# A decoder segment on one core: the small part of every fourth weight chunk formed by an accumulating DMA in SBUF

## The chip, the core and the metric

The kernel runs on one core of a Trainium2 chip. The metric is the time of one execution on the device, in microseconds (us), the median of several runs. The engines are named as the profile names them: PE is the matrix engine TensorE and PEld its weight loads, DVE is VectorE, ACT is ScalarE, POOL is GpSimd; SP is SyncE, which here only issues DMAs. SBUF is the on-chip working memory, PSUM the memory into which PE accumulates.

## The reference, cut to what matters

Two layers work on 256 tokens of 2048 features in float32. Layer 0 mixes tokens with a gated linear recurrence (HGRN2), layer 1 with differential attention over keys and values made from layer 0's output; each is followed by an MLP of 8192 hidden features and a gated embedding:

```python
x = x + o.reshape(b, s, A_WIDTH) @ a_w_out[j]                    # o: HGRN2 mixer, or attention with b_w_out
h = rms_norm(x, ln_mlp[i])
x = x + jnp.square(jax.nn.relu(h @ mlp_up[i])) @ mlp_down[i]
gate = jax.nn.sigmoid(rms_norm(x, ln_ple[i]) @ ple_gate[i])
x = x + gate * (p[i] @ ple_proj[i])
```

With few tokens nearly all the work is matrix products with large float32 weights, each of which is read once.

## The kernel before

The products are made in float32r, a shortened float32, and to keep the accuracy each operand is split into a large part and a small one: `hi` is the value rounded to float32r, and `lo` is the value minus `hi`. A product is then the sum of three: hi times hi, lo times hi and hi times lo.

Weights come in **chunks** of 512 KB, 128 partitions by 1024 elements: two blocks of 128 input features by 512 output features. `chunk` (L91 to L98) brings one: SP loads `raw` (L93), ACT rounds it into `hi` (L96), and DVE subtracts into `lo` (L97). There are four buffers for `raw` and three each for `hi` and `lo`, so a chunk can be prepared only when PE has finished the chunk three before it. 872 chunks are brought in one execution.

`group_b` (L119) takes eight chunks for 512 output features, with the weights stationary. Each chunk serves two pairs of feature blocks, eight matmuls a pair in `mm_b` (L108): for each block, `hi` against both parts of the activations side by side (L114, 512 columns), then `lo` against their large part alone (L116, 256 columns). The second pair starts only when two chunks have gone through the first, so PE takes chunk 0 first pair, chunk 1 first pair, chunk 0 second pair, chunk 1 second pair, and from chunk 2 on both pairs of a chunk. `group_a` (L133) does the same with the tokens stationary, twelve matmuls of 512 columns a chunk (L143 to L145), for the values of the two mixers (four groups of `w_in`, four of `w_v`).

At the end of a group its sums are taken from PSUM. In an up projection (`ev_up`, L523) that is a copy on ACT (L235), an addition and a scaled maximum on DVE (L236, L526), a square on ACT (L527) and the split of the result (L102 on ACT, L103 on DVE). In a down projection it is two additions on DVE (L244, L245). Norms, the mixers and the gates go on beside the stream of chunks, a step after each chunk (`pump`).

No order is written out by hand: a scheduler sorts the program's instructions into one queue for each engine by its own estimate of when each can start, and each engine takes its queue in order. PE thus waits at the first instruction whose operand is not there. POOL has almost nothing to do: constants, masks, four memsets of `accd` (L338) and, once, four loads of 512 KB of `x` (L508).

## Time and profile before

| | before |
|---|---|
| median of 2 runs | 2548.05 us (2545.41 to 2550.69) |
| the profiled execution | span 2545.3 us; no other time is given for it |
| granted PE clock, mean | 0.999 |
| DMA, mean | 184 GB/s, 467.24 MB in all |
| chunks | 872 |

The span runs from the first to the last instruction of one execution taken by the profiler. "Busy" counts an engine's instructions, without waits; a busy PE is not PE at its peak. In rows of waits one reads who waited, for whom, how long in total, how often, and the longest. In rows of the timeline one reads the start, the length, the engine, the line, what is written from what, and in brackets how long the engine had been idle and what ended that. "Landing" is the time from a DMA's issue until its data are there. In rows by stretch, each engine has its busy time and its count, then come PE's granted clock, the share of time that the DMA engines were busy, and GB/s.

### The profile page before, as it was taken

The page shows a single profiled execution, that of the slowest core. Times are in us where ns is not written, and L with a number is a line of the kernel's source. Part 1 is how long each engine was busy: PE and PEld are TensorE (multiplying, and loading weights), DVE is VectorE, ACT ScalarE, POOL GpSimd, SP SyncE. Part 2 cuts the span into 40 slices and gives each one's busy share as a digit, 9 for nine tenths or more (in the row PEclk, how much of TensorE's full clock was granted, in tenths as well). Part 3 has the DMA queues.
Part 4 walks back from the last instruction along what each step waited for, and adds up shares of the span by engine and source line. Part 5 has one row for each costly group of instructions (what it writes and reads, how often), then busy time and mean ns, then how long its engine had stood idle before and what let it go on. Part 6 is the DMA issues. An engine that isn't in the chain of part 4 may idle for free.

```text
span 2545.3 us, 36254 instructions
## 1 busy us (share of the span) xinstructions
PE 2529.0 (99%) x14350; PEld 2199.1 (86%) x14350; DVE 1686.0 (66%) x2064; ACT 1360.0 (53%) x1703; POOL 9.7 (0%) x19
## 2 busy tenths in 40 slices
PE   8999999999999999999999999999999999999998
PEld 7888888888888888888888888888888888888887
DVE  7898887665555555556687686566555555556666
ACT  7666666444344354455576566555435445435555
POOL 0000000000000000000000000000000000000000
PEclk9999999999999999999999999999999999999999
DMA  7555554666666666666656555566666656666665
GB/s 234 173 158 166 165 174 151 214 191 189 190 189 189 187 189 190 191 189 191 183 184 186 179 154 159 169 190 185 187 183 195 185 184 197 187 188 190 190 188 159
DMA packets 128570, 467.24 MB, mean 184 GB/s; under 512 B 14288, under 2 KB 14928, under 8 KB 128400
## 3 DMA queue, kind: packets, MB, share of 16 engines
q1 hardware_dynamic: 127440, 461.95, 59.2%
q0 software_dynamic: 816, 2.89, 0.4%
q8 instruction: 112, 1.84, 0.3%
q14 instruction: 58, 0.48, 0.1%
q10 hardware_dynamic: 144, 0.09, 0.0%
HBM read 462.77 MB, written 2.10 MB: 183 GB/s over the span
## 4 chain that ended last, share of the span: by engine, by line
PE 98%; DVE 1%; DMA 0%; ACT 0%; issue 0%; SPq 0%; ACTq 0%
PE mmps L114 58%; PE mmps L116 29%; PE mmps L145 2%; PE mmps L144 2%; PE mmps L143 2%; PE smps L382 1%; PE mmps L573 1%; PE smps L216 1%; PE mmps L575 0%; DMA xa<-x_t 0%; PE smps L345 0%; PE smps L661 0%; PE smps L689 0%; DVE lo L97 0%; PE smps L413 0%; PE smps L415 0%
## 5 line engine op out<-in xcount | busy, mean ns | idle before, releaser
L114 PE MATMUL mmps<-big,hi 128*128 128x512 f32 x6336 | 2221.7, 395 | 0.1
L116 PE MATMUL mmps<-big,lo 128*128 128x256 f32 x6336 | 1770.1, 279 | 0.4 <-DVE lo L97 0.4
L97 DVE TENSOR_TENSOR lo<-raw,hi 128x1024 fp32r<-128x1024 f32 x872 | 1066.1, 1224 | 796.4 <-ACT hi L96 795.2
L96 ACT CAST hi<-raw 128x1024 fp32r<-128x1024 f32 x872 | 914.1, 1049 | 1005.9 <-PE mmps L114 926.2
L114 PEld LDWEIGHTS mmps<-big,hi 128*128 128x128 f32 x6336 | 1189.4, 188 | 278.8 <-DVE u L236 0.4
L116 PEld LDWEIGHTS mmps<-big,lo 128*128 128x128 f32 x6336 | 1191.1, 188 | 2.5 <-DVE lo L97 0.7
L143 PE MATMUL mmps<-hi,big 128*128 128x512 f32 x256 | 102.3, 399 | 0.0
L144 PE MATMUL mmps<-lo,big 128*128 128x512 f32 x256 | 100.1, 391 | 0.3 <-DVE lo L97 0.3
L145 PE MATMUL mmps<-hi,big 128*128 128x512 f32 x256 | 100.3, 392 | 0.0
L235 ACT COPY t<-mmps 128x512 f32<-128x512 f32 (+1 forms) x114 | 65.1, 572 | 24.0 <-PE mmps L116 22.3
L527 ACT ACTIVATE u<-u 128x512 f32<-128x512 f32 x64 | 40.3, 629 | 48.7 <-DVE u L526 48.7
L145 PEld LDWEIGHTS mmps<-hi,big 128*128 128x128 f32 x256 | 48.1, 188 | 10.3
L144 PEld LDWEIGHTS mmps<-lo,big 128*128 128x128 f32 x256 | 48.2, 188 | 9.7 <-DVE lo L97 0.5
L143 PEld LDWEIGHTS mmps<-hi,big 128*128 128x128 f32 x256 | 48.2, 188 | 9.1
L236 DVE TENSOR_TENSOR u<-mmps,t 128x512 f32<-128x512 f32 x80 | 54.7, 684 | 0.4
L103 DVE TENSOR_TENSOR big<-u,big 128x512 fp32r<-128x512 f32 x80 | 54.7, 683 | 0.2
L244 DVE TENSOR_TENSOR x<-mmps,x 128x512 f32<-128x512 f32 x80 | 54.5, 687 | 0.4
L102 ACT CAST big<-u 128x512 fp32r<-128x512 f32 x80 | 49.4, 618 | 4.8 <-DVE u L423 4.5
L245 DVE TENSOR_TENSOR x<-mmps,x 128x512 f32<-128x512 f32 x80 | 51.2, 680 | 0.0
L526 DVE SCALAR_TENSOR_TENSOR u<-u,rn 128x512 f32<-128x512 f32 x64 | 44.0, 688 | 1.1
L161 ACT ACTIVATE big<-x,sml 128x256 fp32r<-128x256 f32 x96 | 41.0, 498 | 6.4 <-DVE x L245 6.4
L162 DVE SCALAR_TENSOR_TENSOR big<-x,sml,big 128x256 fp32r<-128x256 f32 x96 | 40.2, 481 | 0.0
(157 smaller groups left out, 1067.6 us busy)
## 6 DMA issues: line engine op xcount, KB each, us to landing
raw<-w_up SPq DMA_DIRECT2D x256, 512.0 KB, 4.2
raw<-w_dn SPq DMA_DIRECT2D x256, 512.0 KB, 4.2
raw<-w_in SPq DMA_DIRECT2D x128, 512.0 KB, 3.7
raw<-w_pg SPq DMA_DIRECT2D x56, 512.0 KB, 3.9
raw<-w_ao SPq DMA_DIRECT2D x32, 512.0 KB, 3.8
raw<-w_k SPq DMA_DIRECT2D x32, 512.0 KB, 3.8
raw<-w_q SPq DMA_DIRECT2D x32, 512.0 KB, 3.6
raw<-w_v SPq DMA_DIRECT2D x32, 512.0 KB, 3.6
```

Of the source, the lines that this page charges most:

```text
L96: nc.scalar.copy(hi, raw)
L97: nc.vector.tensor_tensor(lo, raw, hi.bitcast(F32), ALU.subtract)
L103: nc.vector.tensor_tensor(dst[:, k, 1, :], src, dst[:, k, 0, :].bitcast(F32), ALU.subtract)
L114: nc.tensor.matmul(ps[:, ml, :], hi[:, k, m * P:(m + 1) * P], rhs[:, k0 + k].rearrange("p a t -> p (a t)"), start=st, stop=False)
L116: nc.tensor.matmul(ps[:, ml, T:2 * T], lo[:, k, m * P:(m + 1) * P], rhs[:, k0 + k, 0, :], start=False, stop=en)
L143: nc.tensor.matmul(ps[:, tt, :], xs[:, kc, 0, ts], hi[:, k], start=st, stop=False)
L144: nc.tensor.matmul(ps[:, tt, :], xs[:, kc, 0, ts], lo[:, k], start=False, stop=False)
L145: nc.tensor.matmul(ps[:, tt, :], xs[:, kc, 1, ts], hi[:, k], start=False, stop=en)
L235: nc.scalar.copy(t, ps[:, :, T:2 * T])
L236: nc.vector.tensor_tensor(out, ps[:, :, 0:T], t, ALU.add)
L244: nc.vector.tensor_tensor(xm, ps[:, :, 0:T], xm, ALU.add)
L245: nc.vector.tensor_tensor(xm, ps[:, :, T:2 * T], xm, ALU.add)
```

## The change

Three chunks in four stay as they are. For each chunk whose count is a multiple of four, DVE's subtraction is left out. Instead ACT, after rounding `raw` into `hi`, copies `raw` once more with a scale of -1 into `lo`, which leaves minus the rounded value there; then POOL issues a DMA from `raw` to `lo` that adds what it reads to what is there. `lo` ends as `raw` minus `hi`, as before. The DMA reads and writes 128 rows of 4 KB, all within SBUF.

```diff
         lo = wp.tile([P, KCS, CW], F32R, tag="lo", name="lo")
         nc.scalar.copy(hi, raw)
-        nc.vector.tensor_tensor(lo, raw, hi.bitcast(F32), ALU.subtract)
+        turn[0] += 1
+        if turn[0] % 4 == 0:
+            nc.scalar.activation(lo, raw, AF.Copy, scale=-1.0)
+            nc.gpsimd.dma_start(lo.rearrange("p a b -> p (a b)"), raw.rearrange("p a b -> p (a b)"), accum_op=ALU.add)
+        else:
+            nc.vector.tensor_tensor(lo, raw, hi.bitcast(F32), ALU.subtract)
         return hi, lo
 
+    turn = [0]
+
```

The rest of the diff takes comments away. Lines behind the change stand seven further down in the changed kernel: its L102 is the subtraction L97, its L121 and L123 are the matmuls L114 and L116, its L109, L242 and L534 are L102, L235 and L527; L99 is the new copy and L100 the new DMA.

The scheduler makes new queues from this. Three places show what moves. The first is ACT's queue in an up projection, from chunk c=1 of a group to c=4 (each `hi` row is one chunk; the third is c=3). Before:

```order
L96 CAST hi_6758<-raw_6756 128x1024
L235 COPY t_6725<-mmps_6546 128x512
L96 CAST hi_6788<-raw_6786 128x1024
L527 ACTIVATE u_6724<-u_6724 128x512
L235 COPY t_6733<-mmps_6547 128x512
L102 CAST big_6351<-u_6724 128x2x256
L527 ACTIVATE u_6732<-u_6732 128x512
L96 CAST hi_6810<-raw_6808 128x1024
L102 CAST big_6351<-u_6732 128x2x256
L96 CAST hi_6832<-raw_6830 128x1024
```

In the changed kernel, the same chunks:

```order
L96 CAST hi_6819<-raw_6817 128x1024
L242 COPY t_6786<-mmps_6605 128x512
L96 CAST hi_6849<-raw_6847 128x1024
L534 ACTIVATE u_6785<-u_6785 128x512
L242 COPY t_6794<-mmps_6606 128x512
L109 CAST big_6408<-u_6785 128x2x256
L534 ACTIVATE u_6793<-u_6793 128x512
L96 CAST hi_6871<-raw_6869 128x1024
L109 CAST big_6408<-u_6793 128x2x256
L99 ACTIVATE lo_6872<-raw_6869 128x1024
L96 CAST hi_6894<-raw_6892 128x1024
```

The copy into `lo` stands one instruction behind the chunk's `hi`, with the evacuation's last cast between them, and ahead of the next chunk's `hi`.

The second place is PE's queue at the start of the same chunk, c=3 (the numbers of `mmps` are the two pairs of feature blocks). Before:

```order
L114 MATMUL mmps_6740<-big_4048,hi_6810 128x512 [waits Activation_49]
L116 MATMUL mmps_6740<-big_4048,lo_6811 128x256 [waits DVE_49]
L114 MATMUL mmps_6740<-big_4048,hi_6810 128x512
L116 MATMUL mmps_6740<-big_4048,lo_6811 128x256
L114 MATMUL mmps_6740<-big_4048,hi_6810 128x512
```

In the changed kernel:

```order
L121 MATMUL mmps_6801<-big_4081,hi_6871 128x512 [waits Activation_49]
L121 MATMUL mmps_6802<-big_4081,hi_6871 128x512
L123 MATMUL mmps_6801<-big_4081,lo_6872 128x256 [waits DMASW4_49,Activation_49]
L121 MATMUL mmps_6801<-big_4081,hi_6871 128x512
L123 MATMUL mmps_6801<-big_4081,lo_6872 128x256
```

The first use of `lo` now waits for a DMA, and one `hi` matmul of the second pair has been taken ahead of it. At c=7 of a group the order of PE is as before, with one `hi` matmul ahead of the wait.

The third place is SP's queue with the loads of the same stretch (the first row is c=1, the third c=3). Before:

```order
L93 DMA raw_6756<-w_up0 128x1024 [waits DMAHW7_49,DVE_49]
L93 DMA raw_6786<-w_up0 128x1024 [waits DMAHW0_49,DVE_49]
L93 DMA raw_6808<-w_up0 128x1024 [waits DMAHW1_49,DVE_49]
L93 DMA raw_6830<-w_up0 128x1024 [waits DMAHW2_49,DVE_49]
L93 DMA raw_6852<-w_up0 128x1024 [waits DMAHW3_49,DVE_49]
```

In the changed kernel:

```order
L93 DMA raw_6817<-w_up0 128x1024 [waits DMAHW5_49,DMASW2_49]
L93 DMA raw_6847<-w_up0 128x1024 [waits DMAHW0_49,DVE_49]
L93 DMA raw_6869<-w_up0 128x1024 [waits DMAHW2_49,DVE_49]
L93 DMA raw_6892<-w_up0 128x1024 [waits DMAHW1_49,DMASW3_49]
L93 DMA raw_6914<-w_up0 128x1024 [waits DMAHW3_49,DVE_49]
```

The buffer of a chunk whose `lo` is accumulated is given back by the landing of that DMA (DMASW), and the load that takes it is the one five or six chunks later.

## The prediction, made before the result was known

> **What bounds the kernel now.** I read the profile page first: its busy shares, the chain that ended last, and the costliest groups.

> ```profile
> span 2545.3 us, 36254 instructions
> PE 2529.0 (99%) x14350; PEld 2199.1 (86%) x14350; DVE 1686.0 (66%) x2064; ACT 1360.0 (53%) x1703; POOL 9.7 (0%) x19
> ...
> PE 98%; DVE 1%; DMA 0%; ACT 0%; issue 0%; SPq 0%; ACTq 0%
> ...
> L97 DVE TENSOR_TENSOR lo<-raw,hi 128x1024 fp32r<-128x1024 f32 x872 | 1066.1, 1224 | 796.4 <-ACT hi L96 795.2
> L96 ACT CAST hi<-raw 128x1024 fp32r<-128x1024 f32 x872 | 914.1, 1049 | 1005.9 <-PE mmps L114 926.2
> ```

> TensorE (PE) is busy 99% of the span and the chain is PE to 98%. PE is idle for 16 us in all, so no edit that leaves its matmuls alone can win more than 0.6%; VectorE (DVE) and ScalarE (ACT) have room. The waits say who paces whom.

> ```profile
> ACT hi L96 <- PE mmps L114: 926.2, 614, 3.2
> DVE lo L97 <- ACT hi L96: 795.2, 614, 3.6
> ...
> PE mmps L116 <- DVE lo L97: 1.6, 3, 0.9
> ```

> ACT waits for PE 614 times: a chunk's `hi` slot (three of them) must be given back before ACT may round the chunk. DVE waits for ACT. PE itself waits for `lo` 1.6 us in the whole run. So preparation is paced from behind, and what matters is its lead: from the moment a slot comes free to the moment PE needs that chunk's `lo`. The timeline of ACT gives it. First a down projection, where a row of `hi` starts when PE ends the chunk three before:

> ```profile
> 1006.01 1.05 ACT L96 CAST hi<-raw 128x1024 fp32r<-128x1024 f32 x1 [1.72 <-PE mmps L114]
> ...
> 1011.56 1.05 ACT L96 CAST hi<-raw 128x1024 fp32r<-128x1024 f32 x1 [1.72 <-PE mmps L114]
> 1014.33 1.06 ACT L96 CAST hi<-raw 128x1024 fp32r<-128x1024 f32 x1 [1.72 <-PE mmps L114]
> 1018.49 1.05 ACT L96 CAST hi<-raw 128x1024 fp32r<-128x1024 f32 x1 [3.10 <-PE mmps L114]
> 1019.88 1.06 ACT L96 CAST hi<-raw 128x1024 fp32r<-128x1024 f32 x1 [0.33 <-PE mmps L114]
> 1022.65 1.05 ACT L96 CAST hi<-raw 128x1024 fp32r<-128x1024 f32 x1 [1.72 <-PE mmps L114]
> ```

> The one long gap of each group of eight (3.10 us) marks c=3: chunk 0 is given back only after both chunks 0 and 1 went through the first pair of blocks. That tells the rows apart: c=7 starts at 1006.01 and c=3 of the next group at 1018.49. A chunk starts on PE when the chunk before it ends, which is when ACT starts `hi` two chunks later. So c=7 has 1011.56 - 1006.01 = 5.55 us, and c=3 has 1022.65 - 1018.49 = 4.16 us. These two are exactly the chunks whose count is a multiple of four (four chunks of `w_pp` come first, then groups of eight). An up projection has its evacuation on ACT as well:

> ```profile
> 582.72 1.05 ACT L96 CAST hi<-raw 128x1024 fp32r<-128x1024 f32 x1 [1.77 <-PE mmps L114]
> ...
> 588.38 1.05 ACT L96 CAST hi<-raw 128x1024 fp32r<-128x1024 f32 x1 [1.78 <-PE mmps L114]
> ...
> 595.36 0.63 ACT L527 ACTIVATE u<-u 128x512 f32<-128x512 f32 x1 [1.58 <-DVE u L526]
> 595.90 1.04 ACT L96 CAST hi<-raw 128x1024 fp32r<-128x1024 f32 x1
> 596.84 0.61 ACT L102 CAST big<-u 128x512 fp32r<-128x512 f32 x1
> ...
> 599.68 1.05 ACT L96 CAST hi<-raw 128x1024 fp32r<-128x1024 f32 x1 [1.28 <-PE mmps L114]
> ```

> Here c=7 has 588.38 - 582.72 = 5.66 us and c=3 only 599.68 - 595.90 = 3.78 us. PE needs `lo` one `hi` matmul after the chunk's start, and in the changed order two `hi` matmuls after it at c=3; the rows below start 0.23 us apart, so I add 0.23 at c=7 and 0.46 at c=3.

> ```profile
> 1011.48 0.39 PE L114 MATMUL mmps<-big,hi 128*128 128x512 f32 x1
> 1011.71 0.27 PE L116 MATMUL mmps<-big,lo 128*128 128x256 f32 x1
> ```

> **Deadlines** from the start of `hi`: down c=3 4.62, c=7 5.78; up c=3 4.24, c=7 5.89 us.

> **What the change removes.** 218 of the 872 subtractions on DVE, 218 x 1.224 = 267 us of busy time. DVE is not on the path, so this is worth nothing.

> **What it adds on ACT.** 218 copies with scale -1. The nearest row of that shape is the ACTIVATE of 128x1024:

> ```profile
> L225 ACT ACTIVATE pt<-pz x11: 417/1056/1062, 1264.8 to 2539.4; 128x1024 f32<-128x1024 f32 x7, 128x256 f32<-128x256 f32 x4
> ```

> That is 1.06 us, 230 us in all, on an engine that is half idle: no cost by itself. But it stands after `hi` and ahead of the DMA, so it lies on the chunk's path: 1.05 + 1.06 and some 0.03 for handing over, 2.14 us after `hi` starts. In the up projections the changed order has the L102 cast between the two, 0.6 us more at c=3. The next `hi` is pushed back by about 1 us; it has a whole chunk more of lead, and its `lo` on DVE comes 1.2 us behind it, so that delay is hidden.

> **What it adds on POOL and the DMA engines.** 218 accumulating transfers of 512 KB, SBUF to SBUF. No row of this trace shows one; call L the time from its issue on POOL to its landing. The rows around it:

> ```profile
> q1 hardware_dynamic: 127440, 461.95, 59.2%
> ...
> raw<-w_up SPq DMA_DIRECT2D x256, 512.0 KB, 4.2
> raw<-w_v SPq DMA_DIRECT2D x32, 512.0 KB, 3.6
> x<-x_t POOLq DMA_DIRECT2D x4, 512.0 KB, 8.3
> cst<-consts POOLq DMA_DIRECT2D x1, 257.0 KB, 5.2
> ```
> ```profile
> DMA to landing us min/median/max: 3.3/4.0/11.9
> ```
> ```profile
> out<-x SPq DMA_DIRECT2D x1, 512.0 KB, 2.6
> ```
> ```profile
> L508 POOL DMA_DIRECT2D x<-x_t x4: 527/532/536, 445.2 to 446.8; - x4
> ```
> ```profile
> L93 SPq DMA_DIRECT2D raw<-w_up x256: 327/328/328, 508.6 to 2343.3; - x128
> ```

> Lower bound 2.6: a store of 512 KB out of SBUF with nothing beside it. Upper bound 8.3: the loads of `x` from POOL's queue, four at once beside the weights. I take 5.2, built up from the fastest weight load: 3.3 us (the second fence's row is that of all `raw` loads), plus 0.53 - 0.33 = 0.20 for POOL's longer issue, plus one more pass over 512 KB, because an accumulation must also read its destination. The price of a pass: the weight queue's packets took 59.2% of 2545.3 us for 461.95 MB, 3.26 us per MB, 1.71 us for 0.524 MB. The `cst` row, from POOL at half the size, has 5.2 too.

> [...]

> **The lateness.** `lo` is ready 2.14 + L after `hi` starts (2.74 + L for c=3 of an up projection). Less the deadlines: down c=3 L - 2.48, c=7 L - 3.64; up c=3 L - 1.50, c=7 L - 3.75. Nothing behind it on PE can go first, since PE takes its instructions in order, so each is a stall of PE; and the stall also delays the next slot's release, so it is not won back. With L = 5.2: down 2.72 + 1.56 = 4.28 us per group, up 3.70 + 1.45 = 5.15. The token-stationary groups (L143 to L145) take their chunks in plain order:

> ```profile
> 1506.00:1608.00 102.00, 101.93 (x491) 84.25 (x490) 68.03 (x119) 62.32 (x109) 0.00 (x0) 1.00 0.52 161
> ```

> 32 chunks in 102 us, 3.19 each; two chunks and one matmul are 6.61 us of deadline, so L - 4.47 = 0.73, twice a group.

> Groups: the 872 chunks are 107 groups of eight and 16 others. 256 chunks of `w_up` make 32 up groups; 4 groups of `w_in` and 4 of `w_v` are token-stationary; the other 67 I count as down groups. Sum: 67 x 4.28 + 32 x 5.15 + 8 x 1.46 = 286.8 + 164.8 + 11.7 = **463 us**. Against the profiled 2545.3 that is 3008.6; the median of the runs lies 2.7 us above that execution, so **3011 us**.

> **Costed at nothing.** The raw buffer of such a chunk is now freed by the landing, not by DVE. A load five or six chunks later waits for it, and the loads behind it on SP's queue wait too. At the landing PE starts that chunk, so the load has more than three chunks (8.3 us) before its own `hi`, against 4.2 to land; two loads queued behind it are 1.7 us each behind. Were that cover gone, the same stall would pass to `hi`. On POOL the transfers stand behind four memsets of `accd`, which wait for matmuls of heads long since streamed, and behind the four loads of `x`, 2.1 MB at 3.26 us per MB: 7 us once in the run, within the rounding of L.

> **Rivals.** (1) *A copy's price*: the second read overlaps the first and L is 3.3. Then c=7 is in time and c=3 is late by 0.82 and 1.80: 67 x 0.82 + 32 x 1.80 = 113 us, about 2660. For it: the fastest loads; against: both POOL rows. (2) *Not slower*: L at or under 2.68, the point at which 67 x (L - 2.48) + 32 x (L - 1.50) is 51 us, that is 2%. At the bound of 2.6 the sum is 43 us and the time 2591. For it: the lone `out` row; against: SP's issue there is the shorter, it reads once, and DMA engines here are 59% taken. (3) *A slow accumulation*: L = 8.3, lateness down 10.48, up 11.35, token-stationary 7.66 per group: 702 + 363 + 61 = 1127 us, about 3675. For it: the `x` rows; against: those queued four deep. (4) *The clock*: stalls of 3 us and more lower PE's granted clock.

> ```profile
> 2540.00:2545.00 5.00, 0.00 (x0) 0.00 (x0) 1.28 (x3) 1.14 (x3) 0.00 (x0) 0.52 0.07 26
> ```
> ```profile
> 8.57 0.63 PE L114 MATMUL mmps<-pt,hi 128*128 128x512 f32 x1
> 9.00 0.41 PE L116 MATMUL mmps<-pt,lo 128*128 128x256 f32 x1
> 9.21 0.63 PE L114 MATMUL mmps<-pt,hi 128*128 128x512 f32 x1
> ```

> With PE idle at the end, the clock shown is 0.52; after the idle start a pair of matmuls takes 0.64 us instead of 0.35. If c=3 of 99 groups ran slow (2.77 us become 5.07 at worst, but the start was slow for some 3.8 us only, a loss of 1.7): 168 us more, about 3180. Against it: 2.7 to 3.7 us of idleness between long busy stretches. [...]

> **How the numbers follow.** My forecast, L between 4 (2762) and 6.5 (3290), gets 0.55; rival 1, L from 2.7 to 4, 0.17; rival 2, 0.05; rival 3, above 6.5, 0.18; rival 4, 0.05. The range is 2720 (L near 3.8) to 3600 (L near 7.9), which leaves out rival 2, most of rival 1's lower half and the tail of rival 3, some 0.2. About 2% can be told from no change here. Slower by more: everything but rival 2, 0.95; within: 0.04; faster, for which nothing in the profile gives room: 0.01.

> **What would show it.** Right: PE's L116 waits for the DMA of `lo`, two times a group, c=3 about 1.2 us longer than c=7 in down groups and 2.3 in up groups; landing near 5 us; DVE busy near 1420 us, ACT near 1590; clock 1.00. Wrong: no such waits (then L is short), waits on `hi` or on `raw` instead (then the buffers bind), matmuls of 0.63 us in mid-run (the clock), or c=3 and c=7 waits alike.

## The result, and the profile after

| | before | changed |
|---|---|---|
| median of 2 runs | 2548.05 us (2545.41 to 2550.69) | 3125.68 us (3121.60 to 3129.77) |
| ratio, 95% interval | | 1.2273 [1.2219, 1.2328] |
| span of the profiled execution | 2545.3 us | 3119.8 us |
| PE idle (span less busy) | 16.3 us | 419.4 us |
| PE busy | 2529.0 us | 2700.4 us |
| mean granted clock of PE | 1.00 | 0.955 |

The change costs 23%, and the forecast of 3011 us lies 115 us short. The table splits the 574.5 us between the two spans: 403 are PE's idle time and 171 are PE being busy longer with the same 14350 matmuls. The first was forecast, at 463 us; the second was not.

First the page of the changed kernel: busy time of the engines, the two DMA queues (packets, MB, share of 16 engines), the chain that ended last, and the groups that the change touches.

```profile
span 3119.8 us, 37274 instructions
PE 2700.4 (87%) x14350; PEld 2294.5 (74%) x14350; DVE 1448.1 (46%) x1846; ACT 1558.8 (50%) x1921; POOL 197.0 (6%) x237
...
q1 hardware_dynamic: 127440, 461.95, 44.5%
q0 software_dynamic: 32208, 117.19, 20.6%
...
PE 30%; DMA 30%; issue 26%; DVE 7%; ACT 7%; POOLq 0%; ACTq 0%; POOL 0%; SPq 0%; DVEq 0%
...
L121 PE MATMUL mmps<-big,hi 128*128 128x512 f32 x6336 | 2323.1, 409 | 1.6 <-ACT hi L96 1.5
L123 PE MATMUL mmps<-big,lo 128*128 128x256 f32 x6336 | 1832.3, 292 | 389.9 <-DMA lo<-raw 385.9
...
L100 POOL DMA_DIRECT2D lo<-raw x218 | 187.3, 859 | 2882.7 <-ACT lo L99 2590.0
L99 ACT ACTIVATE lo<-raw 128x1024 fp32r<-128x1024 f32 x218 | 229.6, 1053 | 7.9 <-PE mmps L151 7.9
```

The chain that was 98% PE is now 30% DMA. Nearly all idle time of PE (389.9 us) stands before L123, the matmul with `lo`, and its releaser is the new DMA; before L121, the matmul with `hi`, it is 1.6 us. So no `hi` comes late, neither through ACT's longer queue nor through the raw buffers. The queue of the accumulating transfers (with 2.9 MB of others, as before) moves a fifth of the bytes, yet takes 20.6% of the DMA engines against 44.5% for four times as much.

The waits (total, times, longest) and the landing of the new DMA:

```profile
POOL lo L100 <- ACT lo L99: 2590.0, 196, 19.3
...
PE mmps L123 <- DMA lo<-raw: 388.3, 193, 5.1
```
```profile
L100 POOL DMA_DIRECT2D lo<-raw x218: 845/857/901, 20.9 to 3105.1; - x109
...
DMA to landing us min/median/max: 4.5/4.7/6.3
```

193 waits of 2.0 us on average: two for nearly each of the 99 groups with stationary weights. One such chunk, c=3 of a down projection, engine by engine; ACT, POOL, then PE up to the wait of c=7 of the same group.

```profile
1205.05 1.05 ACT L96 CAST hi<-raw 128x1024 fp32r<-128x1024 f32 x1 [3.15 <-PE mmps L121]
1206.01 1.05 ACT L99 ACTIVATE lo<-raw 128x1024 fp32r<-128x1024 f32 x1
```
```profile
1207.35 0.85 POOL L100 DMA_DIRECT2D lo<-raw  x1 [13.12 <-ACT lo L99]
```
```profile
1209.21 0.64 PE L121 MATMUL mmps<-big,hi 128*128 128x512 f32 x2
1212.29 0.35 PE L123 MATMUL mmps<-big,lo 128*128 128x256 f32 x1 [2.44 <-DMA lo<-raw]
1212.48 0.39 PE L121 MATMUL mmps<-big,hi 128*128 128x512 f32 x1
...
1214.23 0.63 PE L121 MATMUL mmps<-big,hi 128*128 128x512 f32 x1
1214.66 0.41 PE L123 MATMUL mmps<-big,lo 128*128 128x256 f32 x1
1214.87 0.63 PE L121 MATMUL mmps<-big,hi 128*128 128x512 f32 x1
...
1226.16 0.36 PE L123 MATMUL mmps<-big,lo 128*128 128x256 f32 x1 [1.20 <-DMA lo<-raw]
1226.36 0.40 PE L121 MATMUL mmps<-big,hi 128*128 128x512 f32 x1
```

Read it as a sum. `hi` starts at 1205.05; POOL begins the DMA 2.30 us later; with the median landing of 4.7 us `lo` is there at about 1212.05; PE goes on at 1212.29, after two `hi` matmuls and a wait of 2.44 us. Then, half a microsecond after the restart, a pair of matmuls takes 0.64 us instead of 0.35, until 1216.3. The windows of the same stretch (us, PE, PEld, DVE, ACT, POOL, then the granted clock) name that: the clock is halved for 3.4 us. After the shorter wait of c=7, 1.20 us, the matmul keeps its 0.40 us.

```profile
1209.20:1212.90 3.70, 1.26 (x8) 0.80 (x7) 1.28 (x2) 1.05 (x1) 0.00 (x0) 1.00 1.01 228
1212.90:1216.30 3.40, 3.40 (x13) 2.91 (x13) 0.00 (x0) 0.08 (x1) 0.00 (x0) 0.50 0.93 292
1216.30:1224.50 8.20, 8.20 (x49) 7.16 (x48) 2.45 (x2) 4.02 (x4) 0.86 (x1) 1.00 0.46 125
```

At c=3 of a group that follows a group of an up projection the wait is longer, since the evacuation of the group before then stands on ACT ahead of the copy. Three waits from the start of the first MLP show it: c=3 of its first group, which follows an output projection and waits like a down group, then c=3 and c=7 of its second group:

```profile
613.73 0.36 PE L123 MATMUL mmps<-big,lo 128*128 128x256 f32 x1 [2.60 <-DMA lo<-raw]
...
641.33 0.36 PE L123 MATMUL mmps<-big,lo 128*128 128x256 f32 x1 [3.48 <-DMA lo<-raw]
653.69 0.36 PE L123 MATMUL mmps<-big,lo 128*128 128x256 f32 x1 [1.06 <-DMA lo<-raw]
```

### The profile page after: what moved, and what is told of

It is laid out like the page before. It is cut to its first block, busy times and chain, and to the rows that moved or that the text cites. A ratio compares the mean times of both kernels' runs of the same rounds, so it can differ in the third digit from the quotient of the medians.

```text
span 3119.8 us, 37274 instructions
## 1 busy us (share of the span) xinstructions
PE 2700.4 (87%) x14350; PEld 2294.5 (74%) x14350; DVE 1448.1 (46%) x1846; ACT 1558.8 (50%) x1921; POOL 197.0 (6%) x237
## 3 DMA queue, kind: packets, MB, share of 16 engines
q1 hardware_dynamic: 127440, 461.95, 44.5%
q0 software_dynamic: 32208, 117.19, 20.6%
## 4 chain that ended last, share of the span: by engine, by line
PE 30%; DMA 30%; issue 26%; DVE 7%; ACT 7%; POOLq 0%; ACTq 0%; POOL 0%; SPq 0%; DVEq 0%
DMA lo<-raw 17%; PE mmps L121 16%; PE mmps L123 9%; DVE lo L102 5%; DMA raw<-w_up 4%; DMA raw<-w_dn 4%; ACT hi L96 4%; ACT lo L99 1%; PE mmps L151 1%; PE mmps L152 1%; DMA raw<-w_in 1%; PE mmps L150 1%; DMA raw<-w_pg 1%; DVE u L533 0%; DVE u L243 0%
## 5 line engine op out<-in xcount | busy, mean ns | idle before, releaser
L121 PE MATMUL mmps<-big,hi 128*128 128x512 f32 x6336 | 2323.1, 409 | 1.6 <-ACT hi L96 1.5
L123 PE MATMUL mmps<-big,lo 128*128 128x256 f32 x6336 | 1832.3, 292 | 389.9 <-DMA lo<-raw 385.9
L123 PEld LDWEIGHTS mmps<-big,lo 128*128 128x128 f32 x6336 | 1256.4, 198 | 465.8 <-issue 287.8
L96 ACT CAST hi<-raw 128x1024 fp32r<-128x1024 f32 x872 | 911.1, 1045 | 1301.6 <-PE mmps L121 1214.4
L121 PEld LDWEIGHTS mmps<-big,hi 128*128 128x128 f32 x6336 | 1236.2, 196 | 279.3 <-ACT hi L96 1.9
L102 DVE TENSOR_TENSOR lo<-raw,hi 128x1024 fp32r<-128x1024 f32 x654 | 799.9, 1224 | 1336.5 <-ACT hi L96 1333.5
L100 POOL DMA_DIRECT2D lo<-raw x218 | 187.3, 859 | 2882.7 <-ACT lo L99 2590.0
L99 ACT ACTIVATE lo<-raw 128x1024 fp32r<-128x1024 f32 x218 | 229.6, 1053 | 7.9 <-PE mmps L151 7.9
L242 ACT COPY t<-mmps 128x512 f32<-128x512 f32 (+1 forms) x114 | 65.1, 572 | 95.7 <-PE mmps L123 92.9
L534 ACT ACTIVATE u<-u 128x512 f32<-128x512 f32 x64 | 40.2, 629 | 48.8 <-DVE u L533 48.8
L109 ACT CAST big<-u 128x512 fp32r<-128x512 f32 x80 | 49.4, 617 | 5.6 <-DVE u L430 5.6
## 6 DMA issues: line engine op xcount, KB each, us to landing
raw<-w_up SPq DMA_DIRECT2D x256, 512.0 KB, 4.5
raw<-w_dn SPq DMA_DIRECT2D x256, 512.0 KB, 4.4
lo<-raw POOLq DMA_DIRECT2D x218, 512.0 KB, 4.7
raw<-w_in SPq DMA_DIRECT2D x128, 512.0 KB, 4.3
raw<-w_pg SPq DMA_DIRECT2D x56, 512.0 KB, 4.3
raw<-w_ao SPq DMA_DIRECT2D x32, 512.0 KB, 4.4
raw<-w_k SPq DMA_DIRECT2D x32, 512.0 KB, 4.4
raw<-w_q SPq DMA_DIRECT2D x32, 512.0 KB, 4.0
```

Source lines behind the costliest of these rows:

```text
L96: nc.scalar.copy(hi, raw)
L99: nc.scalar.activation(lo, raw, AF.Copy, scale=-1.0)
L100: nc.gpsimd.dma_start(lo.rearrange("p a b -> p (a b)"), raw.rearrange("p a b -> p (a b)"), accum_op=ALU.add)
L102: nc.vector.tensor_tensor(lo, raw, hi.bitcast(F32), ALU.subtract)
L121: nc.tensor.matmul(ps[:, ml, :], hi[:, k, m * P:(m + 1) * P], rhs[:, k0 + k].rearrange("p a t -> p (a t)"), start=st, stop=False)
L123: nc.tensor.matmul(ps[:, ml, T:2 * T], lo[:, k, m * P:(m + 1) * P], rhs[:, k0 + k, 0, :], start=False, stop=en)
```

## The experiments

Theory A is the prediction's: a chunk's preparation has a fixed lead, from the release of its slot to PE's first use of `lo`, and the path copy, POOL, DMA is longer than that lead. Rival B: it is the traffic, 114 MB more through the DMA engines beside the weights. Rival C: the copy on ACT and the shifted order of the queues. For the extra busy time: the clock, lowered by the idleness itself, against a cost of the matmuls that has nothing to do with the waits. Each edit is against the changed kernel. Where no interval stands, the time is of one execution; the kernel before had medians of 2545.7 to 2547.1 us beside them.

**e1: DVE adds in the DMA's place.**

```diff
-            nc.gpsimd.dma_start(lo..., raw..., accum_op=ALU.add)
+            nc.vector.tensor_tensor(lo, raw, lo.bitcast(F32), ALU.add)
```

> The copy of minus the large part stays on ACT for every fourth chunk, but DVE adds raw to it instead of the DMA. Theory A (the lead: hi, copy and DMA one after the other take longer than the slots give): copy and addition take 1.05 + 1.23 us behind hi, 3.3 us (3.9 in up projections) against deadlines of 4.2 to 5.9, so no stall: 2545 to 2565 us. Theory B (traffic: 218 more transfers crowd the weight loads): the same. Theory C (the copy on ACT and the changed order of its queue): most of the loss stays, 2900 us or more.

2558.97 us, ratio 1.0048 [1.0032, 1.0065]. The copy is still on ACT (1558.2 us busy) and still ahead of the addition; PE waits for `lo` hardly at all:

```profile
PE 2537.0 (99%) x14350; PEld 2204.6 (86%) x14350; DVE 1686.0 (66%) x2064; ACT 1558.2 (61%) x1921; POOL 9.7 (0%) x19
```
```profile
PE mmps L123 <- DVE lo L100: 1.9, 2, 1.1
```

The copy and its place in ACT's queue cost 0.5%, the DMA the rest. PE's shifted order is not in e1 (two `hi` matmuls in a row stand 6 times in its trace, 112 times in the changed kernel's), but it is in e2b below (112 times), which loses 165 us by all its causes together. So rival C is out as the cause of the loss.

**e2 and e2b: a plain DMA copy.** `accum_op` is removed, so `lo` is `raw` itself and the subtraction is left out for those 218 chunks.

```diff
-            nc.gpsimd.dma_start(lo..., raw..., accum_op=ALU.add)
+            nc.gpsimd.dma_start(lo..., raw...)
```

> The DMA copies raw into lo without adding (lo is then raw, so the small part of every fourth chunk is left out of the computation). Theory A: POOL's issue falls from 0.86 to about 0.53 us and one reading of 512 KB goes (1.3 us), landing about 3.1 us instead of 4.7; stalls at c=3 about 0.9 us in down and 1.9 us in up groups, none at c=7, the clock whole: 2640 to 2700 us. Theory B: the loss shrinks as the DMA engines' time does, by about half, to about 2840 us. If the accumulation itself is not dearer than a copy: 3100 us.

The first time this took 8898.93 us. The matmuls were longer from the first ones on, those before the first changed chunk too, with no wait of PE: the record of a `hi` matmul is 2.8 times as long as in the kernel before (1098 against 395 ns), PE's busy time 3.5 times (8882 against 2529 us).

```profile
L121 PE MATMUL mmps<-big,hi 128*128 128x512 f32 x6336 | 6925.2, 1098 | 0.3 <-ACT hi L96 0.3
```

ACT's rounding and DVE's subtraction kept their 1.05 and 1.22 us, so PE alone was slow. The clock given for this run, 1.00, is no measurement: its trace has no record of the clock, while that of every other run has. A pair of matmuls took 1.26 us (10.71 to 11.97), about twice the 0.64 that it takes at half clock in the changed kernel.

The same program ran again, and beside it one with the same values and no DMA:

> The program of e2 once more (plain copy of raw into lo, the subtraction of every fourth chunk left out). If the 8899 us came from a state of the chip in those two executions: 2640 to 2760 us. If they belong to the program or its values: 8900 us again.

It now took 2711.35 us. The 8899 us belong to those executions and not to the program; what slowed PE there stays open, and nothing is drawn from them. The second run shows what the accumulation itself adds:

```profile
L100 POOL DMA_DIRECT2D lo<-raw x218: 527/527/541, 20.5 to 2696.1; - x109
...
DMA to landing us min/median/max: 2.8/2.9/10.1
```
```profile
PE mmps L123 <- DMA lo<-raw: 106.2, 69, 6.2
```

A plain transfer of the same 512 KB costs POOL 0.53 us instead of 0.86 and lands in 2.9 us instead of 4.7, and the waits fall from 388 to 106 us. By the prediction's formula L = 2.9 gives 67 x 0.42 + 32 x 1.40 = 73 us.

**e10: the same values without a DMA.** `nc.vector.tensor_copy(lo, raw)` in the DMA's place; the subtraction is left out as in e2.

> The same values as in e2 (lo is raw for every fourth chunk, the subtraction left out), but written by DVE: no DMA from POOL. If the slowness of e2 came from the values in the products: 8900 us. If it came from the copying DMA, or from a state of the chip: 2550 to 2570 us, as e1.

2549.77 us. What the values are makes no difference; e2b's 165 us are its transfers.

**e3: the same number of chunks, others of each group** (c=2 and c=6, whose first use is further from the slot's release).

```diff
-        if turn[0] % 4 == 0:
+        if turn[0] % 4 == 3:
```

> The same number of accumulating DMAs, but for the chunks c=2 and c=6 of a group instead of c=3 and c=7. Theory A: both have the long lead (5.55 us), so both stall by about 1.1 us and PE's clock stays at 1.00: 99 groups x 2.1 to 2.2 us, 2755 to 2790 us. Theory B: as many transfers and as many bytes, so as after the change, 3100 us. Theory C: as after the change, 3100 us.

2941.33 us, between what the theories wanted. As many bytes, and 184 us less; the total of the waits for the DMA fell from 388 to 266 us. In the down projections both waits were the 1.0 to 1.2 us that A asks for. In the up projections c=2 still waited 2.3 to 2.7 us, and ACT's timeline shows why:

```profile
607.00 1.05 ACT L96 CAST hi<-raw 128x1024 fp32r<-128x1024 f32 x1 [0.69 <-PE mmps L121]
607.95 0.63 ACT L534 ACTIVATE u<-u 128x512 f32<-128x512 f32 x1
608.48 0.57 ACT L242 COPY t<-mmps 128x512 f32<-128x512 f32 x1
608.95 0.62 ACT L109 CAST big<-u 128x512 fp32r<-128x512 f32 x1
609.47 1.06 ACT L99 ACTIVATE lo<-raw 128x1024 fp32r<-128x1024 f32 x1
```

Three instructions of the evacuation have been put between `hi` and the copy, which starts 2.47 us after `hi` does, where in the changed kernel it is 0.96 in a down group and 1.46 at c=3 behind an up group (633.54 to 635.00). The lead is longer, and so is the path.

**e4: DVE negates** instead of ACT: 0.69 us instead of 1.05, and not behind ACT's evacuation.

```diff
-            nc.scalar.activation(lo, raw, AF.Copy, scale=-1.0)
+            nc.vector.tensor_scalar(lo, raw, -1.0, None, ALU.mult)
```

> DVE instead of ACT writes minus the rounded raw into lo, beside hi and not behind it; the accumulating DMA stays. Theory A: in down groups the DMA is issued 0.8 us earlier, in up groups at c=3 about 1.9 us earlier (no cast and no wait between); the changed order has one hi matmul ahead of lo at c=3 instead of two, 0.23 us back. Waits of PE about 1.9 (down, c=3), 1.8 (up, c=3) and 0.3 us (c=7); 2760 to 2860 us, the spread for how much of the slow clock stays. Theory B: as after the change, 3100 us.

2820.08 us, 306 us less than the changed kernel, as A expected. The DMA is unchanged (landing 4.7), only what stands ahead of it is shorter: c=3 mostly waits 1.4 to 1.6 us in down groups and 1.2 to 1.3 behind up groups (1.9 and 1.8 were expected), and half clock is rarer (21 stretches against 68, a granted clock of 0.984 against 0.955). The output projections and the last three groups of each MLP wait longer, 2.7 to 3.3 us.

```profile
PE mmps L123 <- DMA lo<-raw: 161.7, 123, 5.9
```

**e5: c=7 alone**, every eighth chunk.

```diff
-        if turn[0] % 4 == 0:
+        if turn[0] % 8 == 4:
```

> Accumulating DMAs for c=7 alone, half as many. Theory A: 99 stalls of about 1.06 us, clock 1.00: 2645 to 2670 us. Theory B: half of the loss, about 2835 us. Theory C: half of the loss, about 2835 us.

2769.79 us, 100 us above what was expected. The edit does not choose c=7 all through: four single chunks of the gated embedding come between groups of the second MLP and shift the count, and behind them the chosen chunk is c=3. The first MLP, where it is c=7, lost 47 us over 32 groups, waits of 1.0 to 1.2 us each; the second, with c=7 in its first twelve groups and c=3 in its last seventeen, lost 102. Half the transfers thus cost 223 us of 574, and where in the group they fall sets the price.

**e6: PE kept busy while it waits.** Eight matmuls with a zero operand, which add nothing, after the first `hi` matmul of c=3, in 96 groups: 768 x 0.23 = 177 us of busy time put into the stall (`zero` is a strip of zeros, `warm` is 8 there and 0 elsewhere).

```diff
+                if ml == 0 and k == 0:
+                    for _ in range(warm):
+                        nc.tensor.matmul(ps[:, ml, :], hi[...], zero[...], start=False, stop=False)
```

> As the change, but at c=3 PE multiplies by zeros eight times (8 x 0.23 us, results unchanged) after the hi matmul that stands ahead of the wait for lo. If idleness of PE at c=3 is what lowers its clock, the waits get shorter by these 1.8 us, the matmuls run at full speed, and the time falls by most of the 171 us that the matmuls took longer: 2960 to 3010 us. If the slow clock has another cause (the transfers, the number of stalls at all), or the slow matmuls were only a sign and cost nothing: 3120 us or more.

3053.09 us: 73 us faster with 768 matmuls more, though 43 us above the expected band. The page's busy times, then PE at the end of a stall (in this kernel's numbering L123 takes `hi` and L129 `lo`):

```profile
PE 2772.4 (91%) x15118; PEld 2361.3 (77%) x15118; DVE 1449.2 (47%) x1847; ACT 1558.1 (51%) x1921; POOL 196.8 (6%) x237
```
```profile
752.71 0.36 PE L129 MATMUL mmps<-big,lo 128*128 128x256 f32 x1 [1.09 <-DMA lo<-raw]
752.90 0.39 PE L123 MATMUL mmps<-big,hi 128*128 128x512 f32 x1
```

Without the zeros PE is busy 2772 - 177 = 2595 us, 105 less than in the changed kernel. What is left of the wait is 1.09 us here, and the next matmul runs at full speed. Counted over the trace, 15 stretches at half speed (55 us) remain of 68 (281 us). PE's idle time is 278.6 us instead of 419.4: 141 us less, so 36 of the 177 us did not fit into the waits. The transfers are all still there, and the time at half speed fell to a fifth: in these two runs the slow clock went with PE's idleness and not with the transfers.

**e7: DVE subtracts in place, then a plain copy.** The work is as in the reference; the DMA only copies.

```diff
-            nc.scalar.activation(lo, raw, AF.Copy, scale=-1.0)
-            nc.gpsimd.dma_start(lo..., raw..., accum_op=ALU.add)
+            nc.vector.tensor_tensor(raw, raw, hi.bitcast(F32), ALU.subtract)
+            nc.gpsimd.dma_start(lo..., raw...)
```

> DVE subtracts hi from raw in place and POOL's DMA copies the result into lo, no accumulation and no copy on ACT; the data are those of before. Theory A: landing of a plain copy 2.9 us, DVE 1.23 us behind hi: 5.25 us (some 0.6 more in up groups) against 4.6 and 4.2 at c=3 and 5.8 at c=7; waits 0.6 and 1.6 us at c=3, none at c=7, clock near 1.00: 2630 to 2720 us. Theory B (traffic): the DMA engines' time for the copies is about half of that for the accumulations, so about half of the loss, 2840 us. And if the slowness of e2 belongs to a plain copy from POOL into this buffer: 8000 us or more.

2757.7 us, 38 above the band. The landing is the expected 2.9 us, but c=3 mostly waits 1.2 to 1.6 us, in down groups too, for which 0.6 was expected: DVE's subtraction ends at 803.85 + 1.22 = 805.07 and POOL begins its DMA only at 805.60, 0.53 us later. That is not DVE's doing: in e4, where POOL also waits for DVE, the step takes 0.29 us as it does behind ACT. In e7 POOL has a second wait instruction behind the one for DVE; whether that is the reason was not tried. The landing, then DVE and POOL at that place:

```profile
L100 POOL DMA_DIRECT2D lo<-raw x218: 530/530/539, 20.7 to 2742.8; - x109
...
DMA to landing us min/median/max: 2.8/2.9/9.0
```
```profile
803.85 1.22 DVE L99 TENSOR_TENSOR raw<-raw,hi 128x1024 f32<-128x1024 f32 x1 [1.64 <-ACT hi L96]
```
```profile
805.60 0.53 POOL L100 DMA_DIRECT2D lo<-raw  x1 [12.68 <-DVE raw L99]
```

**e8: a fourth buffer for `hi` and `lo` during the two MLPs** (`wh[0]` is a pool of its own, opened anew with four buffers around each MLP; the other stages keep three).

```diff
-        hi = wp.tile([P, KCS, CW], F32R, tag="hi", name="hi")
-        lo = wp.tile([P, KCS, CW], F32R, tag="lo", name="lo")
+        hi = wh[0].tile([P, KCS, CW], F32R, tag="hi", name="hi")
+        lo = wh[0].tile([P, KCS, CW], F32R, tag="lo", name="lo")
```

> As the change, but with four buffers for hi and for lo in both MLPs (three elsewhere, as before). Theory A: one chunk more of lead (2.8 us) covers every stall of the MLPs but some 0.5 us at c=3 of up groups; the MLPs, which the change made longer by 193 and 191 us, come back to about their old length: 2740 to 2800 us in all. Theory B: buffers change nothing in the traffic: 3100 us.

2789.11 us. The two MLPs lost some 20 us each against the kernel before, where the changed kernel lost 194 and 191; the stages that keep three buffers lost as much as they did (some 200 us here, 189 there). The window inside the first MLP, with the copy, the accumulating DMA and its 4.7 us all in place; behind it the kernel before in its own:

```profile
640.00:1300.00 660.00, 659.13 (x3736) 572.32 (x3736) 308.81 (x330) 352.50 (x394) 49.94 (x58) 1.00 0.79 232
```
```profile
512.00:1220.00 708.00, 708.00 (x4065) 618.99 (x4064) 416.40 (x442) 327.25 (x376) 0.00 (x0) 1.00 0.62 188
```

PE is idle 0.9 us in 660, at the full clock, and the matmul records come at 5.66 a microsecond, in the kernel before at 5.74, 1.4% more. The DMA engines are busier than in any stage of the kernel before, 0.79 against 0.56 to 0.62. ACT waits for a weight load 12 times in this window, 26 us in all, and none of it reaches PE. This rejects B: more traffic in the same time costs at most that 1.4% once the lead is a chunk longer.

**e9 and e11: the shortest path I could find with three buffers.** DVE negates, on c=2 and c=6 (e9) or on c=0 and c=4 (e11).

```diff
-        if turn[0] % 4 == 0:
-            nc.scalar.activation(lo, raw, AF.Copy, scale=-1.0)
+        if turn[0] % 4 == 3:
+            nc.vector.tensor_scalar(lo, raw, -1.0, None, ALU.mult)
```

> Two of the shortenings together: the chunks c=2 and c=6, and DVE writing minus the rounded raw beside hi. Theory A: 0.75 us for the copy and 4.7 us of landing against deadlines of 5.8 us, so hardly a wait left in the MLPs and short ones where DVE is busy (up groups, mixers): 2550 to 2640 us, PE's clock 1.00. It can't be faster than before, since PE's own work is unchanged. Theory B (traffic, as many transfers as after the change): a clear loss stays, 2800 us or more.

2812.33 us, ratio 1.1038 [1.1018, 1.1058]: A's number failed. The copy of c=2 has moved behind the evacuation of the down projection on DVE and starts 2.4 us after the evacuation does:

```profile
694.10 1.32 DVE L251 TENSOR_TENSOR x<-mmps,x 128x512 f32<-128x512 f32 x2
695.34 1.28 DVE L252 TENSOR_TENSOR x<-mmps,x 128x512 f32<-128x512 f32 x2
696.53 0.68 DVE L99 TENSOR_SCALAR lo<-raw 128x1024 fp32r<-128x1024 f32 x1
```

For e11 the condition is `turn[0] % 4 == 1`.

> As e9, but for the chunks c=0 and c=4. Theory A with the queue of DVE: in e9 the copy at c=2 stood behind the evacuation of the group before, on DVE (2.7 us in down groups), and that is where its waits in the MLPs came from; at c=0 and c=4 no evacuation stands ahead, both have the long lead, and the MLPs come back to within 15 us each of before, against 80 and 87 us more in e9. In all 2590 to 2670 us, the rest from the mixers and gates. Theory B (traffic): as e9, 2812 us.

2817.42 us, ratio 1.1073 [1.1055, 1.1091]: failed as well. At c=4 the copy stands on DVE behind the subtraction of c=3, which waits for that chunk's late `hi`:

```profile
704.24 1.23 DVE L102 TENSOR_TENSOR lo<-raw,hi 128x1024 fp32r<-128x1024 f32 x1 [2.46 <-ACT hi L96]
705.38 0.69 DVE L99 TENSOR_SCALAR lo<-raw 128x1024 fp32r<-128x1024 f32 x1
```

B's numbers for these two were met, but not by its mechanism: in both, the waits of PE that the trace names are again for the landing of `lo` (152.2 us in 133 waits, and 175.2 in 129), and the MLPs of e8 carry the same traffic almost without waits. What fell is a part of A: that the copy goes when its `raw` is there: the scheduler's place for it in ACT's or DVE's queue decides, and I had not read that ahead. A choice of chunks that hides 4.7 us with three buffers was not found. None of these kernels beats the kernel before, whose PE has only 16 us of idle time to give.

## Why the prediction was right in sign and 115 us short

- **Subtractions off DVE are worth nothing: right.** DVE fell to 1448 us busy (about 1420 forecast) and the time rose. The subtraction kept its 1224 ns.
- **The copy on ACT: right.** 1053 ns (1.06 forecast), ACT 1558.8 us busy (1590). e1 has it in place and loses 0.5%.
- **Raw buffers, SP's queue and POOL's other work at nothing: right.** PE waits 1.6 us before L121, and the new DMAs on POOL wait for ACT 2590 us in all, not for POOL.
- **The deadlines: right.** With the measured landing of 4.7 us the formula gives 2.22 and 1.06 us in down groups, 3.20 and 0.95 in up groups; measured were mostly 2.4 to 2.6 and 1.0 to 1.2, 3.5 and 1.0. The difference between c=3 and c=7, forecast at 1.2 and 2.3, was 1.2 (2.44 and 1.20) and 2.4 (3.48 and 1.06). What sets a group's deadline is the evacuation of the group before it: the 32 with the short one are not the 32 up groups, as counted in the forecast, but 24 of these and 8 down groups that follow one, so the sum is the same by good fortune. The e8 run, with one chunk more of lead, is the direct test: the stalls are gone.
- **L = 5.2: the mis-sized term, by 0.5.** I built it as 3.3 + 0.20 + 1.71. A plain copy within SBUF lands in 2.9 us, not 3.3 (e2b, e7). The accumulation adds 0.33 us on POOL and some 1.5 behind it. The second pass was too dear too: by the queues' rows the accumulating queue takes 20.6% of 3119.8 us for 117.19 MB, 5.5 us per MB, the weight queue 44.5% for 461.95 MB, 3.0; for 0.524 MB that is 2.9 against 1.6 us, a difference of 1.3 and not 1.71. Against the plain copies of e2b (12.1% of 2709.6 us for the same bytes, 2.8 us per MB) it is 1.4, near the 1.5 by which the landing grew behind POOL. With L = 4.7 the sum is 67 x 3.28 + 32 x 4.15 + 8 x 0.46 = 356 us instead of 463.
- **Measured idle time: 403 us more than before.** The 47 us beyond 356 are partly the handing over to POOL, which I had at 0.03 us and which the rows above put at 0.29: the waits at c=3 exceed the formula by 0.22 us in down and 0.3 in up groups, 67 x 0.22 + 32 x 0.3 = 24 us. The rest was not separated in full; the seven whole groups of the gates, counted as plain down groups, have 33 us of waits where the formula gives 7 x 3.28 = 23.
- **The clock: the step that failed.** I priced it at 168 us and then set it aside as a rival with 0.05, because stalls of 2.7 to 3.7 us between long busy stretches seemed short to me; that such stalls leave the clock alone no trace showed. Measured: PE busy 171 us longer, and matmuls of 0.63 us in mid-run, the forecast's own sign against itself. In the 68 stretches at half speed, 281 us in all, 377 `hi` matmuls take 0.42 us from one start to the next instead of 0.23 and 443 `lo` matmuls 0.22 instead of 0.12: 116 us; e6 wins 105 back. Most of the rest lies at the edges of the waits. In the stall above, the two `hi` matmuls ahead of the wait count 0.64 us where in a running stretch they take 2 x 0.23, and the first `lo` matmul after it takes 0.19 (1212.29 to 1212.48) where it has 0.12; over the trace that is some 45 us. So each stall costs about 0.25 us more than the wait that the profile shows. The slow clock was no alternative to the stalls but their consequence, and its price belonged into the sum: 463 us too much by 60 and 171 left out make the 115 that were short (111 between the spans, the rest the two medians' distance from them). That the two errors have opposite signs is luck: with the measured landing of 4.7 us the forecast would have been 356 us on 2548, about 2904, and 222 short.

PE's waits in the changed kernel's trace by their length, and how many of them were followed by a stretch at half speed:

| wait, us | 0.5 to 1.8 | 1.8 to 2.3 | 2.3 to 2.8 | 2.8 to 3.3 | 3.3 to 4 |
|---|---|---|---|---|---|
| waits | 113 | 6 | 40 | 12 | 33 |
| then at half speed | 3 | 2 | 24 | 8 | 30 |

The table has no sharp limit, and length is not all that tells these waits apart. The trace's 136 records of the clock all begin on one grid of 3.413 us (to within 1 ns), so PE's busy time can be counted in each window of that grid. Two waits of the same length (us, PE, PEld, DVE, ACT, POOL, granted clock, DMA, GB/s; the first window holds the whole wait that ends at 1212.29, the other two share the one that ends at 1268.32):

```profile
1209.52:1212.93 3.41, 0.97 (x6) 0.63 (x5) 1.22 (x1) 0.82 (x1) 0.00 (x0) 1.00 1.00 229
...
1264.13:1267.55 3.42, 1.78 (x10) 1.20 (x8) 2.31 (x2) 1.05 (x1) 0.15 (x1) 1.00 0.88 153
1267.55:1270.96 3.41, 2.64 (x15) 2.37 (x16) 0.12 (x1) 0.09 (x1) 0.00 (x0) 1.00 0.81 249
```
```profile
1268.32 0.36 PE L123 MATMUL mmps<-big,lo 128*128 128x256 f32 x1 [2.41 <-DMA lo<-raw]
```

In the window of the wait of 2.44 us PE was busy 28%, and half clock followed; the wait of 2.41 us is cut by the grid into windows that are 52% and 77% busy, and the clock stayed whole. Of all windows at full clock from the first record of the clock on, the 66 in which PE was busy less than 44% were all followed by half clock, 1 of the 16 between 44% and 50%, and none of the 745 above. A window at half clock with PE busy more than 80% was followed by the full clock in 67 of 70 cases here, one with less in none of 11. These are counts of one trace; that they hold for another kernel was not shown.

Of the rivals, a copy's price, "not slower" and the slow accumulation fell by the landing of 4.7 us, which lies inside the forecast's own band of 4 to 6.5.

## What to carry to other kernels

Before moving a step to another queue, measure its lead, from the event that releases its input to the instruction that first uses its output, for each position in the group; an engine that is mostly idle can still be too slow by 2 us at one position, and an in-order consumer makes a stall of each such case. Then look in whose queue the new instruction really stands, since what is ahead of it there adds to its path. If the stalls come out as long as those that half clock followed here (24 of 40 between 2.3 and 2.8 us, 3 of 113 under 1.8), add the matrix engine's slower clock after them to the sum, and see first whether one more buffer of lead makes them go away.
